# Padding the moving operands of the merge and of both MLP products by 64 bytes

## The chip, the cores and the metric

The kernel runs on one core of a Trainium2 chip. The metric is the device time of one execution in microseconds; lower is better. The time before is 3025.41 us, the median of 3 runs (3019.31 to 3026.27).

## The reference

One decoder layer on a sequence of 512 tokens with 2048 channels, in float32. What matters here is its dense part:

```
gates  = sigmoid(z[..., o_gate:] + gate_bias)            # three gates of 2048 channels
merged = g_a*(y_a @ wu[:768]) + g_b*(y_b @ wu[768:1408]) + g_c*(y_c @ wu[1408:])
x = x + merged @ w_out                                   # 2048 x 2048
h = rmsnorm(x, norm_mlp)
x = x + square(relu(h @ mlp_w1)) @ mlp_w2                # 2048 -> 8192 -> 2048
return rmsnorm(x, final_norm)
```

Ahead of it stand an input projection and three token mixers (S5, RWKV-7, gated linear attention), which the change doesn't touch.

## The kernel before, in words

Activations lie transposed, channels on the 128 partitions and the 512 tokens in the free direction, so that a weight tile of 128 x 128 is the standing operand of TensorE and an activation tile the moving one. Every operand of a dense product is split in two float32r tiles, a high part and the rest (`hl`, lines 875 to 877: ScalarE casts, VectorE subtracts). A product of two such pairs is three matmuls: high weights by high activations, high weights by low activations, low weights by high activations (`gemm`, L749 to L751, and `w1_mm`, L802). TensorE's order is the order of the program (`manual_schedule`); the other engines and the queue of SyncE, which issues the loads, are put in order by a planner.

The stages that the change touches come last:

- **The merge** (`up`): 16 output blocks of 16 weight tiles, moving operands `yh`/`yl`, 512 columns. 768 matmuls. The product with `w_out` (`wo`) follows, also 768, from tiles `mh`/`ml` that the change leaves alone.
- **The first MLP product** is done with seven quarter products in place of eight, numbered 1, 5, 6, 3, 7, 2, 4, on 256 columns: 32 units of seven products of 24 matmuls. The moving operands of 1, 5, 6 and 3 lie in one pair of tiles `hA` of the form [128, 8, 4, 256]: for each of 8 blocks k of channels the four operands side by side. They are written while `w_out` runs. Those of 7, 2 and 4 (`hB7`, `hB2`, `hB4`) are tiles of their own, filled at the start of this stage from DRAM through the staging tag `hraw` (L1264): six loads of 512 KB, each split by ScalarE and VectorE.
- **The second MLP product** (`w`): 8 chunks c of the hidden layer, each with 16 output blocks of 8 weight tiles. Its moving operands are `ah`/`al`, each a tile of 1024 columns that holds two operands; tag with 8 buffers, of which a chunk uses four. 2880 matmuls of 512 columns, and at the end 384 of 256.

A step in the free direction is 4 bytes, so a tile of 512 columns is 2048 bytes in each partition. In the program before every tile size above is a multiple of 512 bytes, hence all operands of a stage begin at the same remainder modulo 512. The program's addresses are: weights `whi`/`wlo` at 288, and a weight tile inside begins at a multiple of 512 behind it; `yh`, `yl`, `mh`, `ml`, `uh`, `ul` and the `hB` tiles at 288 too; `hA`, `ah`, `al` and the small tiles `tw`, `ta` of the RWKV preparation (L761 to L763) at 480. The distance of the moving operand's begin from the standing operand's is therefore 0 modulo 512 for `up`, `wo`, `z`, `gt` and `hB`, and 192 for `hA`, `w`, `pw` and `pa`.

Of the kernel before, what the change touches and what calls it, by code (L numbers as in the profile page):

```python
# [7 lines left out]
F32 = mybir.dt.float32  # L8
F32R = mybir.dt.float32r
# [4 lines left out]
P = 128  # L14
T = 512
# [705 lines left out]
class Trunk(K):  # L721
# [181 lines left out]
    def main(self, d, out):  # L903
# [8 lines left out]
        with tc.tile_pool(name="const", bufs=1) as cp, \  # L912
# [9 lines left out]
            def mixpool(name, side=None):  # L922
                return tc.tile_pool(name=name, bufs=1, reuse_waits="tile", side=side)
# [18 lines left out]
            with tc.manual_schedule(engines={mybir.EngineType.PE}):  # L942

                R = cp.tile([P, T], F32, name="R")
                u = []
# [143 lines left out]
                with mixpool("s5a") as sp, mixpool("rprep") as rp:  # L1089
# [14 lines left out]
                    for q in range(2):  # L1104
# [3 lines left out]
                        t = dr.tile([P, T], F32, name=f"tgd{q}")  # L1108
# [47 lines left out]
                m = []  # L1156
                with mixpool("merge") as mp:

                    yt = {j: [mp.tile([P, T], F32R, name=f"y{q}{j}") for q in "hl"] for j in (0, 1, 2, 3, 4, 5, 13, 14, 15)}
                    g0 = [mp.tile([P, T], F32, name=f"gl0_{q}", tag=f"gl{q}", bufs=2) for q in range(3)]  # L1160
                    yy = []
                    for j in list(range(6, NT)) + list(range(6)):
                        t = mp.tile([P, T], F32, name=f"yt{j}", tag="yt", bufs=4)
                        nc.sync.dma_start(t, yd[j])
                        if j not in yt:
                            yt[j] = [mp.tile([P, T], F32R, name=f"y{q}{j}") for q in "hl"]
                        self.hl(t, *yt[j])
                        yy.append(yt[j])
                    for j in range(NT):
                        gt = []  # L1170
                        for q in range(3):
                            t = mp.tile([P, T], F32, name=f"gl{j}_{q}", tag=f"gl{q}", bufs=2) if j else g0[q]
                            nc.sync.dma_start(t, gd[3 * j + q])
                            gt.append(t)
                        pp = [self.ps(f"up{j}_{q}") for q in range(3)]
                        self.run(self.gemm(f"up{j}", d["w_up"][j], [(pp[1], 5), (pp[2], 5), (pp[0], 6)], yy))
                        for q in (1, 2, 0):
                            self.mul(gt[q], gt[q], pp[q])
                        self.add(gt[1], gt[1], gt[2], nc.gpsimd)
                        self.add(gt[0], gt[0], gt[1])  # L1180
                        hi = ap.tile([P, T], F32R, name=f"mh{j}", tag="act")
                        lo = ap.tile([P, T], F32R, name=f"ml{j}", tag="act")
                        self.hl(gt[0], hi, lo)
                        m.append((hi, lo))
# [1 line left out]
                HA = (1, 5, 6, 3)  # L1186
                upper, front = contextlib.ExitStack(), contextlib.ExitStack()
                hp = upper.enter_context(mixpool("hcu", "right"))
                hA = [hp.tile([P, 8, 4, 256], F32R, name=f"hA{q}") for q in "hl"]
                hc = {i: [t[:, :, n] for t in hA] for n, i in enumerate(HA)}  # L1190
                fp = front.enter_context(mixpool("front", "right"))
                x1d = [dr.tile([P, T], F32, name=f"x1d{j}") for j in range(NT)]
# [43 lines left out]
                mp = lower.enter_context(mixpool("w1"))  # L1236
# [20 lines left out]
                with mixpool("hraw", "right") as rp:  # L1257
                    for n, i in ((2, 4), (1, 2), (0, 7)):
                        hc[i] = [mp.tile([P, 8, 256], F32R, name=f"hB{i}{q}") for q in "hl"]
                    for n, i in enumerate((7, 2, 4)):  # L1260
                        with tc.high_priority(self.wprio):
                            for h in range(2):
                                t = rp.tile([P, 4, 256], F32, name=f"hraw{i}{h}", tag="hraw", bufs=3)
                                nc.sync.dma_start(t, d3[:, n, 4 * h:4 * h + 4])  # L1264
                                self.hl(t, *(q[:, 4 * h:4 * h + 4] for q in hc[i]))
                    for n, (i, *w) in enumerate(gen):
                        self.w1_mm(bank[self.BANK[i]], i, w, hc, range(8))
                        self.w1_out(0, i, bank, keep, mp, R2, hid)
                        if n == 1:
                            pm = self.gps("pms")  # L1270
                            nc.tensor.matmul(pm, self.onesD, acc, start=True, stop=True)
                            self.ts(R2, pm, 1e-6, ALU.add)
                            nc.vector.reciprocal(R2, R2)
# [9 lines left out]
                with contextlib.ExitStack() as st:  # L1283
                    mp, hp = (st.enter_context(mixpool(n)) for n in ("x1b", "nrm"))
                    self.stg = st.enter_context(tc.tile_pool(name="sq", bufs=3, reuse_waits="tile"))
                    sq2 = hp.tile([P, T], F32, name="sq2")
                    gap = st.enter_context(mixpool("gap"))
                    gap.tile([P, 20 * 256], F32, name="gap")
                    rp = st.enter_context(mixpool("hr"))
                    xp = st.enter_context(mixpool("ah", "right"))  # L1290
                    acc2 = hp.tile([P, T], F32, name="acc2")
# [2 lines left out]
                    def hidden(u):  # L1294

                        with tc.high_priority(2 * self.wprio):
                            t = rp.tile([P, 1024], F32, name=f"hr{u}", tag="hr", bufs=3)
                            nc.sync.dma_start(t, hid[u])
                            r = [xp.tile([P, 1024], F32R, name=f"a{q}{u}", tag=f"a{q}", bufs=8) for q in "hl"]
                            self.hl(t, *r)  # L1300
                        return [tuple(x[:, T * q:T * q + T] for x in r) for q in range(2)]
                    nxt = [a for u in range(4) for a in hidden(u)]
                    xq = [mp.tile([P, 4, T], F32, name=f"x1b{j}") for j in range(NT // 4)]
                    x1 = [xq[j // 4][:, j % 4] for j in range(NT)]
# [7 lines left out]
                    for c in range(8):  # L1312
                        aa, nxt = nxt, []

                        pts = [bank8(f"w2_{c}_{j}") for j in range(2)]
                        gens = [self.gemm(f"w2_{c}_{j}", d["w2"][c, j], [(pts[j], 8)], aa) for j in range(2)]
                        for gen in gens:
                            for _ in range(3):
                                next(gen)
                        for j in range(NT if c < 7 else NT // 2):  # L1320
                            if j < 2:
                                pt = pts[j]
                                self.run(gens[j])
                            else:
                                pt = bank8(f"w2_{c}_{j}")
                                self.run(self.gemm(f"w2_{c}_{j}", d["w2"][c, j], [(pt, 8)], aa))
                            self.add(x1[j], x1[j], pt)
                            if c < 7 and j in (2, 4, 6, 8):
                                nxt += hidden(4 * c + 3 + j // 2)
                            if c == 7:  # L1330
                                self.sumsq(acc2, x1[j], j)
                                nc.scalar.activation(x1[j], x1[j], AF.Copy, scale=col("final", j))
# [130 lines left out]
```

## Time and profile before

| | |
|---|---|
| median of 3 runs | 3025.41 us |
| profiled execution, its own time | 3027.89 us |
| its span, first to last instruction | 3025.8 us |
| TensorE matmul busy | 2957.4 us (98%) |
| TensorE weight load busy | 2518.7 us (83%), overlaps the matmuls |
| VectorE / ScalarE / GpSimd busy | 61% / 38% / 11% |
| mean granted clock of TensorE | 0.987 |

A matmul's duration in the profile contains what it shares with its neighbours, as they are pipelined: a row says 0.39 us where the next one begins 0.23 us later. What a matmul costs in a row of them is the distance between two starts, called pitch here.

### The profile page before, as it was taken

Reading aid. Unit: us, or ns where it says so; the run is one execution under the profiler, and the core shown is the slowest. Engines: PE = TensorE matmul, PEld = TensorE weight load, DVE = VectorE, ACT = ScalarE, POOL = GpSimd, SP = SyncE. Lnnn points to the kernel's source line nnn. Section 1 sums busy time; section 2 is a strip of 40 time slices with the busy share of each in tenths; the row PEclk is TensorE's granted clock in tenths of the full one; section 3 lists DMA queues with packets and bytes.
Section 4 is the critical chain, followed back from the end, with each engine's and each line's share of the span. In section 5 each row is a group of like instructions: output and inputs, shape, how many; then the busy total and the mean of one; then the engine's idle time right before and its main releaser. Section 6 shows DMA issues by size and latency. Waiting matters only on the chain.

```text
span 3025.8 us, 41943 instructions
## 1 busy us (share of the span) xinstructions
PE 2957.4 (98%) x16447; PEld 2518.7 (83%) x16447; DVE 1830.8 (61%) x2574; ACT 1160.5 (38%) x1434; POOL 325.8 (11%) x560
## 2 busy tenths in 40 slices
PE   8999989899999999999999999999999999999997
PEld 7888777778877777888888999999998888888887
DVE  7766888855673554655445877777775434333436
ACT  6554222234563142432233555555554222222225
POOL 1001666630000000001011000000000000000002
PEclk9999989999999999999999999999999999999999
DMA  5345433445337262655554644454546333233224
GB/s 183 126 162 176 125 105 96 127 130 168 103 98 192 72 175 69 228 168 170 158 162 151 218 160 161 161 168 161 168 141 236 118 125 112 104 118 125 98 98 146
DMA packets 195605, 436.08 MB, mean 144 GB/s; under 512 B 66096, under 2 KB 80176, under 8 KB 194608
## 3 DMA queue, kind: packets, MB, share of 16 engines
q1 hardware_dynamic: 195408, 433.40, 44.4%
q8 instruction: 129, 2.11, 0.3%
q14 instruction: 68, 0.56, 0.1%
HBM read 359.70 MB, written 68.70 MB: 142 GB/s over the span
## 4 chain that ended last, share of the span: by engine, by line
PE 84%; DVE 7%; POOL 3%; DMA 2%; issue 2%; SPq 1%; ACT 1%; DVEq 0%; ACTq 0%; POOLq 0%
PE ha L802 12%; PE w L749 8%; PE w L750 8%; PE w L751 8%; PE hc L802 6%; PE gt L749 6%; PE gt L751 5%; PE gt L750 5%; PE hb L802 3%; PE z L749 2%; PE z L751 2%; PE z L750 2%; PE wo L750 2%; PE up L751 2%; PE up L750 2%; PE wo L749 2%
## 5 line engine op out<-in xcount | busy, mean ns | idle before, releaser
L751 PE MATMUL w<-ah,wlw 128*128 128x512 f32 (+1 forms) x1088 | 413.9, 380 | 1.2 <-DVE wlw L33 1.2
L749 PE MATMUL w<-ah,whw 128*128 128x512 f32 (+1 forms) x1088 | 413.8, 380 | 0.0
L750 PE MATMUL w<-al,whw 128*128 128x512 f32 (+1 forms) x1088 | 413.6, 380 | 0.0
L732 ACT CAST whw<-wrw 128x1024 fp32r<-128x1024 f32 x136 | 142.5, 1048 | 495.1 <-PE w L750 493.5
L30 DVE TENSOR_TENSOR x1b<-x1b,w 128x512 f32<-128x512 f32 (+1 forms) x136 | 89.1, 655 | 384.8 <-PE w L751 375.2
L749 PE MATMUL gt<-uh,whgt 128*128 128x512 f32 x768 | 311.7, 406 | 1.2 <-DVE gz L27 1.2
L751 PE MATMUL gt<-uh,wlgt 128*128 128x512 f32 x768 | 301.4, 392 | 3.6 <-DVE wlgt L33 3.6
L750 PE MATMUL gt<-ul,whgt 128*128 128x512 f32 x768 | 301.1, 392 | 0.0
L749 PE MATMUL z<-uh,whin 128*128 128x512 f32 x608 | 244.6, 402 | 10.3 <-DVE zs L27 10.3
L751 PE MATMUL z<-uh,wlin 128*128 128x512 f32 x608 | 241.6, 397 | 8.1 <-DVE wlin L33 8.1
L751 PEld LDWEIGHTS w<-ah,wlw 128*128 128x128 f32 x1088 | 203.6, 187 | 46.1 <-DVE wlw L33 1.6
L750 PE MATMUL z<-ul,whin 128*128 128x512 f32 x608 | 240.8, 396 | 0.0
L749 PEld LDWEIGHTS w<-ah,whw 128*128 128x128 f32 x1088 | 203.6, 187 | 44.5
L750 PEld LDWEIGHTS w<-al,whw 128*128 128x128 f32 x1088 | 203.6, 187 | 44.5
L732 ACT CAST whgt<-wrgt 128x1024 fp32r<-128x1024 f32 x96 | 100.2, 1046 | 271.0 <-PE gt L750 162.9
L793 ACT CAST whu<-wAu 128x1024 fp32r<-128x1024 f32 x128 | 133.7, 1045 | 159.3 <-DVE wAu L30 82.5
L33 DVE TENSOR_TENSOR wlu<-wAu,whu 128x1024 fp32r<-128x1024 f32 x128 | 156.4, 1222 | 44.9 <-ACT whu L793 44.9
L33 DVE TENSOR_TENSOR wlw<-wrw,whw 128x1024 fp32r<-128x1024 f32 x136 | 168.7, 1241 | 20.5 <-ACT whw L732 20.5
L751 PEld LDWEIGHTS gt<-uh,wlgt 128*128 128x128 f32 x768 | 145.0, 189 | 36.7 <-DVE wlgt L33 5.3
L749 PEld LDWEIGHTS gt<-uh,whgt 128*128 128x128 f32 x768 | 144.8, 189 | 36.5 <-issue 2.5
L750 PEld LDWEIGHTS gt<-ul,whgt 128*128 128x128 f32 x768 | 145.2, 189 | 27.2
L30 POOL TENSOR_TENSOR acc<-acc,sq 128x512 f32<-128x512 f32 x14 | 22.9, 1635 | 1327.3 <-ACT sq L896 1297.2
(495 smaller groups left out, 7061.8 us busy)
## 6 DMA issues: line engine op xcount, KB each, us to landing
wrw<-in_w SPq DMA_DIRECT2D x136, 512.0 KB, 3.2
wrgt<-in_w_in SPq DMA_DIRECT2D x96, 512.0 KB, 4.3
wrin<-in_w_in SPq DMA_DIRECT2D x76, 512.0 KB, 3.9
wrup<-in_w_up SPq DMA_DIRECT2D x32, 512.0 KB, 4.3
wrwo<-in_w_out SPq DMA_DIRECT2D x32, 512.0 KB, 3.9
wAu<-in_w SPq DMA_DIRECT2D x32, 512.0 KB, 5.5
wDu<-in_w SPq DMA_DIRECT2D x32, 512.0 KB, 3.8
wBu<-in_w SPq DMA_DIRECT2D x32, 512.0 KB, 4.3
```

The lines of the kernel that those rows point to most:

```text
L30: (eng or self.nc.vector).tensor_tensor(out, a, b, ALU.add)
L33: (eng or self.nc.vector).tensor_tensor(out, a, b, ALU.subtract)
L732: nc.scalar.copy(hi, raw)
L749: nc.tensor.matmul(ps, hi[:, ws], xh, start=first, stop=False)
L750: nc.tensor.matmul(ps, hi[:, ws], xl, start=False, stop=False)
L751: nc.tensor.matmul(ps, lo[:, ws], xh, start=False, stop=last)
L793: nc.scalar.copy(hi, x)
L802: self.nc.tensor.matmul(ps, w[a][:, ws], hc[i][b][:, k], start=i in (1, 5, 2) and k == 0 and q == 0, stop=k == 7 and q == 2, skip_group_ch ...
```

## The change

The moving operands get 16 unused columns (64 bytes) behind them. The tiles of the merge become 512 + 16 columns long, `hA`'s inner rows 256 + 16, and `ah`/`al` 1024 + 16. Whatever reads or writes them sees the same columns as before. As neighbours now lie at steps of 2112, 1088 and 4160 bytes, which leave 64 modulo 512, the operands of a stage begin at up to eight remainders modulo 512 in steps of 64. For the room, the staging tag `hraw` goes from 3 buffers to 2, and the unused tile `gap`, which only sets where the following pool begins, shrinks by 1 KB in each partition.

```diff
-                    yt = {j: [mp.tile([P, T], F32R, name=f"y{q}{j}") for q in "hl"] for j in (0, 1, 2, 3, 4, 5, 13, 14, 15)}
+                    shifted = lambda j: [mp.tile([P, T + 16], F32R, name=f"y{q}{j}")[:, 0:T] for q in "hl"]
+                    yt = {j: shifted(j) for j in (0, 1, 2, 3, 4, 5, 13, 14, 15)}
...
-                            yt[j] = [mp.tile([P, T], F32R, name=f"y{q}{j}") for q in "hl"]
+                            yt[j] = shifted(j)
...
-                hA = [hp.tile([P, 8, 4, 256], F32R, name=f"hA{q}") for q in "hl"]
+                hA = [hp.tile([P, 8, 4, 272], F32R, name=f"hA{q}")[:, :, :, 0:256] for q in "hl"]
...
-                                t = rp.tile([P, 4, 256], F32, name=f"hraw{i}{h}", tag="hraw", bufs=3)
+                                t = rp.tile([P, 4, 256], F32, name=f"hraw{i}{h}", tag="hraw", bufs=2)
...
-                    gap.tile([P, 20 * 256], F32, name="gap")
+                    gap.tile([P, 19 * 256], F32, name="gap")
...
-                            r = [xp.tile([P, 1024], F32R, name=f"a{q}{u}", tag=f"a{q}", bufs=8) for q in "hl"]
+                            r = [xp.tile([P, 1040], F32R, name=f"a{q}{u}", tag=f"a{q}", bufs=8)[:, 0:1024] for q in "hl"]
```

## Rows read from the trace of the kernel before

**Rows 1.** The page: engines' busy time, the granted clock, the chain by engine.
```profile
PE 2957.4 (98%) x16447; PEld 2518.7 (83%) x16447; DVE 1830.8 (61%) x2574; ACT 1160.5 (38%) x1434; POOL 325.8 (11%) x560
...
PEclk9999989999999999999999999999999999999999
...
PE 84%; DVE 7%; POOL 3%; DMA 2%; issue 2%; SPq 1%; ACT 1%; DVEq 0%; ACTq 0%; POOLq 0%
```

**Rows 2.** Busy time by stretch: merge, first product, second product, its end; (x) counts instructions.
```profile
1303.50:1477.60 174.10, 174.10 (x769) 144.14 (x768) 88.82 (x110) 43.67 (x48) 20.43 (x16) 1.00 0.52 162
1652.00:2290.00 638.00, 630.33 (x5385) 628.13 (x5384) 505.25 (x495) 343.14 (x427) 1.45 (x1) 1.00 0.50 167
2290.00:2962.00 672.00, 672.00 (x2884) 538.61 (x2883) 263.18 (x271) 167.03 (x167) 9.55 (x6) 1.00 0.36 124
2962.00:3011.00 49.00, 45.52 (x389) 44.47 (x387) 36.67 (x49) 33.31 (x53) 16.30 (x9) 1.00 0.48 161
```

**Rows 3.** Timeline of TensorE, single matmuls: start, duration, line, tiles.
```profile
1304.66 0.39 PE L749 MATMUL up<-yh,whup 128*128 128x512 f32 x1
...
1310.79 0.39 PE L749 MATMUL up<-yh,whup 128*128 128x512 f32 x1
...
2102.58 0.28 PE L802 MATMUL hc<-hAh,whu 128*128 128x256 f32 x1
...
2105.30 0.28 PE L802 MATMUL ha<-hB7h,whu 128*128 128x256 f32 x1
...
2108.16 0.28 PE L802 MATMUL hb<-hB2h,whu 128*128 128x256 f32 x1
...
2111.04 0.28 PE L802 MATMUL ha<-hB4h,whu 128*128 128x256 f32 x1
...
2113.92 0.29 PE L802 MATMUL ha<-hAh,whu 128*128 128x256 f32 x1
...
2116.66 0.28 PE L802 MATMUL hc<-hAh,whu 128*128 128x256 f32 x1
...
2399.74 0.39 PE L750 MATMUL w<-al,whw 128*128 128x512 f32 x1
...
2405.81 0.39 PE L749 MATMUL w<-ah,whw 128*128 128x512 f32 x1
```

**Rows 4.** Timeline of TensorE where two small products stand between input products.
```profile
95.60 0.39 PE L750 MATMUL z<-ul,whin 128*128 128x512 f32 x1
...
96.05 0.39 PE L761 MATMUL pw<-twh,whwa 128*128 128x512 f32 x1
...
97.45 0.39 PE L749 MATMUL z<-uh,whin 128*128 128x512 f32 x1
...
98.61 0.39 PE L751 MATMUL z<-uh,wlin 128*128 128x512 f32 x1
...
99.97 0.39 PE L751 MATMUL z<-uh,wlin 128*128 128x512 f32 x1
```

**Rows 5.** The tile hraw: its loads, and their time to landing.
```profile
L1264 SPq DMA_DIRECT2D hraw<-d x6: 319/326/423, 1657.7 to 1669.9; - x6
...
DMA to landing us min/median/max: 4.0/8.0/11.1
```

**Rows 6.** Timeline of SyncE's queue and of VectorE at the first product's start.
```profile
1657.70 2.09 SPq L1264 DMA_DIRECT2D hraw<-d  x3
...
1664.05 3.95 SPq L1264 DMA_DIRECT2D hraw<-d  x2
...
1669.94 0.32 SPq L1264 DMA_DIRECT2D hraw<-d  x1
...
1680.10 2.35 DVE L33 TENSOR_TENSOR hB4l<-hraw,hB4h 128x1024 fp32r<-128x1024 f32 x2
```

**Rows 7.** Whom TensorE waited for, in all: total us, times, longest.
```profile
PE hb L802 <- ACT whu L793: 3.3, 1, 3.3
...
PE ha L802 <- DVE hB4l L33: 0.2, 1, 0.2
```

## The prediction

> **What bounds the kernel now.** I read the page first. TensorE's matmuls are busy for 98% of the span and have 84% of the chain that ended last, and its granted clock is full in nearly every slice [rows 1]. So a change counts only as far as it moves TensorE's pitch or makes it wait. Next come the stages that the diff touches, in the view by stretches [rows 2]: the merge holds 769 matmuls in 174.1 us and the second product 2884 in 672.0 us, both with TensorE busy throughout, and the first product 5385 in 638.0 us with under 8 us idle. [...] No load, cast or eviction ends last there; the pitch itself is the cost.
>
> Then the single matmuls [rows 3]. They show that matmuls of one shape don't have one pitch:
>
> - `up`, 512 columns, distance 0: 1304.66 to 1310.79 is 27 steps, 226.9 ns each (the stretch in [rows 2] gives 226.4).
> - `w`, 512 columns, distance 192: 2399.74 to 2405.81 is 26 steps, 233.4 ns.
> - `hc` from `hA`, 256 columns, distance 192: 2102.58 to 2105.30 is 24 steps, 113.3 ns.
> - `hB2`, 256 columns, distance 0: 2108.16 to 2111.04 is 24 steps, 120.0 ns.
>
> Shape, engine, clock and the weights' addresses are the same inside each pair; what differs is where the moving operand begins against the standing one. So the distance is worth 6.7 ns a matmul, and with opposite sign for the two widths: 192 is the bad one for 512 columns and the good one for 256. Whether that is a matter of both addresses or of the moving one alone can't be told here, since all weights begin at one remainder.
>
> [rows 4] show what a change of distance does on the way. Input products run at distance 0; then six matmuls `pw`, `pa` at distance 192 (96.05 to 97.45) take 1.40 us, 233.3 ns each from the first on; back at distance 0 the next five take 1.16 us (97.45 to 98.61), 232 ns each, and only then does the pitch fall to 226.7 ns (six in 98.61 to 99.97). A run at the other distance is thus entered at once, while the way back to 0 costs about five matmuls.
>
> **The change part by part.** After it, the operands of a stage begin at 0, 64, ..., 448 modulo 512. The trace holds just 0 and 192 in long runs. I assume that what counts is the distance modulo 128, so that even multiples of 64 behave as 0 and odd ones as 192. That is a choice: it is the shortest period in which the two measured kinds differ on this grid. No run of matmuls in these rows lies under 226.7 ns at 512 columns or 113.3 at 256, so no stage is let go below that, and a stage that has it today can only lose.
>
> *Merge, 768 matmuls.* `yh` now begins at even multiples, `yl` at odd ones, so each triple goes 0, 64, 0. It leaves the best pitch known for 512 columns. Lower end: 226.7 as now, 0 us. Upper end: 233.4, 768 x 6.7 ns = 5.1 us. Since the distance changes with every matmul, I take the pitch of the five that follow a change, nearly 231 to 232: 768 x 4.3 ns = +3.3 us.
>
> *First product, 3072 matmuls on `hA`.* Operand n of block k begins at 192 + 64n + 256k: products 1 and 6 (n = 0, 2) keep the good kind, 5 and 3 (n = 1, 3) get the bad one, for all 24 matmuls of a product. What such a run costs behind one at 192 stands in [rows 3]: `hB7`, 2105.30 to 2108.16, is 24 steps of 119.2 ns. So 1536 x 5.9 ns = 9.1 us. Product 7, which then follows one of its own kind, goes from 119.2 to 120.0: 768 x 0.8 = 0.6 us. Product 6, now entered from the bad kind, is what product 1 is today: 2113.92 to 2116.66, 24 steps of 114.2 ns against 113.3, 768 x 0.9 = 0.7 us. Sum +10.4 us. Lower end 0 us (all new distances as good as 192), upper end 3072 x 6.7 = +20.6 us. `hB2`, `hB7` and `hB4`, which have the bad distance today, aren't touched.
>
> *Second product, 2880 matmuls.* Buffer b of `ah` and of `al` is shifted by 64b alike, so six matmuls in a row share a distance and the kind alternates with each buffer. It leaves the bad distance. If the half that becomes good were good at once, 1440 x 6.7 ns = -9.6 us. With the five slow ones of [rows 4] in each run of six, that run takes 1.16 + 0.227 = 1.387 us in place of 1.400, only 2.2 ns a matmul: 1440 x 2.2 = -3.2 us. I take the middle, -6.4 us. Outer ends: 0 us, and -19.3 us if all eight distances gave 226.7.
>
> *Its end, 384 matmuls of 256 columns* (the last stretch of [rows 2]), distance 192 today, half of them turned bad: 192 x 6.7 = +1.3 us; ends 0 and +2.6.
>
> *`hraw` from 3 buffers to 2.* Before, the first three loads go out together at 1657.70, the fourth and fifth behind the release of a buffer at 1664.05 and after, the sixth at 1669.94 [rows 6]; a load lands 4.0 to 11.1 us after its issue [rows 5]. With two buffers the third waits for the first release, 1664.05, so some 5 us later, and the last two follow it. [...] The last splits end at 1682.45 today (1680.10 + 2.35 [rows 6]), and TensorE waits 0.2 us for them [rows 7]: there is no cover left at that end. What hides part of it is the 3.3 us wait for weights just ahead [rows 7], in which the third operand isn't wanted either. Ends: -3.3 us if the later loads let those weights land sooner and that wait goes, and +6 us if the whole delay shows; I take +2 us, near the cover.
>
> *Nothing for the rest.* The same casts and subtractions write the same columns. On `hA` three blocks of 256 lie 1088 bytes apart in place of 1024, beside the `w_out` product, where VectorE and ScalarE have room [rows 1]; if that cover were gone, the delay could show only in the first waits of the first product. `gap` issues no instruction.
>
> Sum: 3.3 + 10.4 - 6.4 + 1.3 + 2.0 = +10.6 us. The profiled execution took 3027.89 us, 2.1 more than its span and 2.5 above the median shown; it becomes 3038.5, and on the median 3036.0.
>
> [...]
>
> **The rivals.**
>
> *The distance is not what sets the pitch.* The 6.7 ns could come from something that the stages differ in besides (which tiles, which engines write next to them, the number of weight loads in flight). For it: no run of the trace has the same tiles at two distances. Against it: `pw`, `pa` change to 233.3 ns in the midst of input products and back. Time: only `hraw`, 3025.4 + 2.0 = 3027. Chance 0.20.
>
> *Most new distances are good for both widths* (the faster side). Only one remainder in eight would be bad for a width: 192 for 512 columns, 0 for 256. Then seven eighths of `w` drop to 226.7, 2520 x 6.7 = -16.9 us; an eighth of `up` gets worse, +0.6; an eighth of `hA`, +2.6; end +0.3; `hraw` +2. Sum -11.4, 3014. It decides from the point where `w` averages below about 229.4 ns, as then its gain passes 11.5 us, and `hA` stays below 116. For it: the trace knows six remainders on the grid not at all. Against it: entering 0 from 192 costs five slow matmuls even where 0 is good. Chance 0.18.
>
> *Many distances never settle.* Each change of distance starts the slow steps anew, `hA` goes to the 120.0 ns of `hB` throughout and `up` to 233.4, while `w` gains nothing: 20.6 + 5.1 + 2.6 + 2 = +30, 3055. For it: the five slow matmuls. Against it: entering 192 costs nothing. Chance 0.10.
>
> The forecast has 0.52: its own range is 3028 to 3045, from `w` at -9.6 or -3.2, `hraw` at 0 or 6, and half as much on `hA`.
>
> **How the numbers follow.** A measurement of this kernel tells some 0.3%, 9 us, from no change: 3016 to 3034.5 counts as the same. Faster: the second rival's 0.18 nearly whole, 0.16. Same: the first rival's 0.20, and about a third of the forecast, where `hA` costs less, in all 0.38. Slower: the rest of the forecast and the third rival, 0.46. The range for 8 in 10 takes in the first rival, most of the second and the near part of the third: 3011 to 3049.
>
> **What would show it.** In the changed trace: `w` averaging 230 to 232 ns a matmul (the same stretch near 666 us in place of 672); `up` near 231; `ha`/`hc` of products 5 and 3 at 119 to 120 with 1 and 6 at 113 to 114; the waits of `hb` and `ha` on `hraw`'s splits longer by some 2 us. The prediction is wrong in its assumption if products 5 and 3 differ between even and odd k, or if 1 and 6 move; wrong in its sign if `w` falls to 227 while `hA` stays at 113.

## The result, and the profile after

The changed kernel takes 3057.49 us (median of 4 runs, 3055.87 to 3059.69) against 3024.23 of the kernel before, measured beside it. The ratio is 1.0113, with a 95% interval of 1.0095 to 1.013: 33 us slower. Slower was the forecast too, but by less: 3036.0 us, with a range that ended at 3049.

The page of the profiled execution (span 3054.0 us, its own time 3055.87), with the lines that answer to [rows 1]:

```profile
PE 2972.4 (97%) x16447; PEld 2536.6 (83%) x16447; DVE 1831.3 (60%) x2574; ACT 1160.7 (38%) x1434; POOL 326.1 (11%) x560
...
PE 83%; DVE 7%; DMA 3%; POOL 3%; issue 2%; SPq 1%; ACT 1%; DVEq 0%; ACTq 0%; POOLq 0%
```

The instructions are the same in number. TensorE's matmuls are busy 15.0 us longer, the span is 28.2 us longer: about half of the loss is longer matmuls, half is waiting. The view by stretches places it. Each stretch is cut at the first matmul of its stage; the columns are the stretch, its length, the busy time of TensorE's matmuls, of its weight loads, of VectorE, ScalarE and GpSimd, the granted clock and the DMA share with GB/s. The kernel before, cut finer than [rows 2] (unit 0 of the first product, units 1 to 30, the last unit, the second product):

```profile
1652.83:1684.22 31.39, 23.72 (x172) 21.72 (x170) 26.67 (x27) 15.61 (x20) 1.45 (x1) 0.95 0.72 256
1684.22:2270.08 585.86, 585.86 (x5042) 585.86 (x5041) 461.23 (x451) 314.00 (x391) 0.00 (x0) 1.00 0.49 163
2270.08:2289.60 19.52, 19.52 (x170) 19.52 (x169) 16.94 (x18) 13.19 (x16) 0.00 (x0) 1.00 0.48 163
2289.60:2961.61 672.01, 672.01 (x2882) 538.57 (x2881) 263.39 (x270) 166.98 (x167) 9.55 (x6) 1.00 0.36 124
```

The changed kernel, the merge ahead of these four:

```profile
1301.34:1478.95 177.61, 177.61 (x770) 144.11 (x769) 88.84 (x110) 43.53 (x48) 20.58 (x16) 1.00 0.51 159
1653.07:1690.42 37.35, 26.58 (x172) 24.19 (x170) 29.23 (x29) 16.30 (x20) 1.46 (x1) 0.86 0.66 229
1690.42:2287.62 597.20, 597.20 (x5043) 597.20 (x5041) 458.79 (x449) 312.97 (x390) 0.00 (x0) 1.00 0.47 156
2287.62:2318.63 31.01, 20.07 (x171) 19.86 (x169) 16.98 (x18) 14.91 (x18) 0.00 (x0) 0.88 0.54 187
2318.63:2989.30 670.67, 670.20 (x2880) 542.74 (x2881) 263.85 (x270) 166.25 (x165) 9.96 (x6) 1.00 0.36 123
```

Merge and units 1 to 30 are longer with TensorE busy throughout: that is pitch. Unit 0 and the last unit hold idle time, 10.8 and 10.9 us, where they had 7.7 and none. The last unit's matmuls end after 20.07 us; the idle time behind them counts to its stretch, which ends where the second product begins. That stretch is the surprise: nothing was forecast there. The waits of TensorE name what ends each (total us, times, longest; they answer to [rows 7]):

```profile
PE w L749 <- ACT ah L876: 10.9, 1, 10.9
...
PE hb L802 <- ACT hB2h L876: 2.6, 1, 2.6
PE hb L802 <- DVE hB2l L33: 2.1, 1, 2.1
...
PE ha L802 <- ACT hB4h L876: 1.3, 1, 1.3
...
PE ha L802 <- DVE hB4l L33: 0.9, 1, 0.9
```

The first is new: the second product's first matmul waits 10.9 us for the cast of its first operand. That cast waits for a load of the hidden layer, `hr<-hid`, line 1299 after and 1298 before. SyncE's queue in the kernel before (two more loads go at 1710.67 and 1730.19, so that the three buffers of `hr` are filled long ahead; the loads at 2285.04 fill them again):

```profile
1691.87 0.33 SPq L1298 DMA_DIRECT2D hr<-hid  x1
...
2285.04 2.92 SPq L1298 DMA_DIRECT2D hr<-hid  x3
...
2298.16 0.32 SPq L828 DMA_DIRECT2D hid<-hy  x1
```

and in the changed one, where no such load stands ahead of 2312.80:

```profile
2291.67 0.33 SPq L828 DMA_DIRECT2D hid<-hy  x1
2296.21 14.05 SPq L729 DMA_DIRECT2D wrw<-in_w  x6
2312.38 0.33 SPq L828 DMA_DIRECT2D hid<-hy  x1
2312.80 1.77 SPq L1299 DMA_DIRECT2D hr<-hid  x3
```

Before, the loads of the first chunk go out ahead of the last store of the hidden layer, `hid<-hy`, and TensorE doesn't wait for their casts. After, they stand behind that store, which needs the last unit's results: what was a prefetch, three of its four loads over 550 us early, comes after its consumer is free.

The wait costs more than its length. In the first 6.37 us of the second product, behind the 10.9 us of idling, the granted clock is 0.51:

```profile
2318.63:2325.00 6.37, 5.90 (x13) 4.32 (x14) 3.65 (x3) 2.09 (x2) 0.00 (x0) 0.51 1.05 397
```

Most matmuls begin 427 ns apart there, and the first 24 take 3.4 us more than in the run below that has the same paddings without the wait.

The same boundaries give this table (us, change against the kernel before; the three columns on the right are experiments told below). The product with `w_out` is unchanged to 0.1 in all of them.

| stage | forecast | changed kernel | paddings of merge and second product alone | padded `hA`, `hraw` at 2 | `gap` alone |
|---|---|---|---|---|---|
| merge | +3.3 | +3.52 | +3.52 | 0 | 0 |
| first product, unit 0 | +2.0 | +5.95 | -0.17 | +3.33 | -0.49 |
| units 1 to 30 | +10.4 | +11.34 | 0 | +11.33 | -0.01 |
| last unit | 0 | +11.49 | 0 | +0.38 | +11.31 |
| second product | -6.4 | -1.33 | -4.69 | +2.51 | +2.61 |
| its end | +1.3 | +0.55 | +0.57 | +1.02 | +0.96 |

The changed stages together are 31.5 us longer. The gate product, which the change doesn't touch, was 3.5 us shorter in this profiled execution than in that of before; over the runs below it lies between 735.5 and 741.6. That is why the two profiled executions differ by only 28 us.

The columns don't add up stage by stage. The three experiments together give 2.67 us for unit 0 and 2.55 for the end, where the changed kernel has 5.95 and 0.55. The end also moved by 0.96 with `gap` alone, where no operand of TensorE moved.

### The profile page after: what moved, and what is told of

Its sections match the earlier page's. It is cut to its first block, busy times and chain, and to the rows that moved or that the text cites. A ratio compares the mean times of both kernels' runs of the same rounds, so it can differ in the third digit from the quotient of the medians.

```text
span 3054.0 us, 41951 instructions
## 1 busy us (share of the span) xinstructions
PE 2972.4 (97%) x16447; PEld 2536.6 (83%) x16447; DVE 1831.3 (60%) x2574; ACT 1160.7 (38%) x1434; POOL 326.1 (11%) x560
## 4 chain that ended last, share of the span: by engine, by line
PE 83%; DVE 7%; DMA 3%; POOL 3%; issue 2%; SPq 1%; ACT 1%; DVEq 0%; ACTq 0%; POOLq 0%
PE ha L802 12%; PE w L750 8%; PE w L749 8%; PE w L751 8%; PE hc L802 6%; PE gt L749 5%; PE gt L751 5%; PE gt L750 5%; PE hb L802 3%; PE z L749 2%; PE z L751 2%; PE z L750 2%; PE up L751 2%; PE up L750 2%; PE up L749 2%; PE wo L750 2%
## 5 line engine op out<-in xcount | busy, mean ns | idle before, releaser
L749 PE MATMUL w<-ah,whw 128*128 128x512 f32 (+1 forms) x1088 | 415.3, 382 | 10.9 <-ACT ah L876 10.9
```

Source lines behind the costliest of these rows:

```text
L749: nc.tensor.matmul(ps, hi[:, ws], xh, start=first, stop=False)
```

## The experiments

**The unused tile alone.** The kernel before, with nothing but this:

```diff
-                    gap.tile([P, 20 * 256], F32, name="gap")
+                    gap.tile([P, 19 * 256], F32, name="gap")
```

> The kernel before with one edit: the unused tile gap 1 KB smaller, so that the buffers hr of the second product begin 1 KB lower and the first of them lies on a buffer of pk6, which the first product's last unit still reads. No operand of TensorE moves. Theory A (the lost prefetch): the loads of hr for the first chunk go out only behind that read, TensorE waits some 11 us before the first matmul of w; 12 to 16 us slower than before. Theory B (the late loads come from hA's growth, which pushes the tile wA under the third buffer of hr, and gap is harmless): within 2 us of before, and no wait over 1 us at the start of w.

3039.3 us (3037.08 to 3042.99, 4 runs) against 3026.45 (13 runs), ratio 1.0045 [1.003, 1.006]. The last unit is 11.31 us longer, the second product 2.61, and the wait is the one of the changed kernel:

```profile
PE w L749 <- ACT ah L876: 11.2, 1, 11.2
```

So theory A holds: a tile that no instruction touches costs 13 us by its size. By the program's addresses, `gap` ends where the three buffers of `hr` begin: at 133408 before, at 132384 after. There the second buffer of `pk6` lies (132384 to 133408), a copy that the last unit of the first product still reads. What holds the load back at last is its place in SyncE's queue. In the changed kernel VectorE's last read of `pk6` begins at 2299.1 and takes 0.4 us:

```profile
L33 DVE TENSOR_TENSOR hy<-hc,pk x32: 415/424/425, 1670.4 to 2299.1; 128x256 f32<-128x256 f32 x32
```

The load goes out 13 us later, at 2312.80, 0.1 us after the queue is done with the last store (2312.38 and 0.33 long). The overlap moved the load to another place in the queue's order, which the planner sets; why this is behind the store and not only behind the read isn't shown. The 2.61 us in the second product lie in its first 24 matmuls, as above.

**The staging tag alone.** The kernel before, with:

```diff
-                                t = rp.tile([P, 4, 256], F32, name=f"hraw{i}{h}", tag="hraw", bufs=3)
+                                t = rp.tile([P, 4, 256], F32, name=f"hraw{i}{h}", tag="hraw", bufs=2)
```

> The kernel before with one edit: hraw with 2 buffers in place of 3. Theory A: this alone makes the first unit of the first product 5 to 6 us longer, through waits of hb and ha for hB2 and hB4; 3029 to 3031 us on the median. Theory B (the waits in the changed kernel come from its slower matmuls and other order): under 2 us.

3031.18 us (10 runs), ratio 1.0012 [1.0003, 1.0021]; unit 0 is 3.52 us longer, the other stages of the table unchanged to 0.3. In unit 0 neither number was met: more than B's, less than A's; the median lies 4.7 us up, at A's upper end, with an interval of 0.9 to 6.4. The waits are A's: TensorE now waits 6.3 us for the splits of `hB2` and `hB4`, partly in place of other waits. The longest new wait is this one (the kernel before has no row for it):

```profile
PE hb L802 <- ACT hB2h L876: 3.8, 1, 3.8
```

**The unused tile put back.** The changed kernel, with `gap` at 20 * 256 again:

```diff
-                    gap.tile([P, 19 * 256], F32, name="gap")
+                    gap.tile([P, 20 * 256], F32, name="gap")
```

> The changed kernel with one edit back: gap at its old size. hr then begins behind pk6 again, but its third buffer still lies on wA, which hA's growth pushed down. Theory A (gap alone lost the prefetch): the wait of 10.9 us at the start of w goes, 11 to 15 us faster than the changed kernel, 3042 to 3046. Theory B (wA's overlap is enough to lose it): as the changed kernel, 3055 to 3060.

3046.63 us (4 runs), ratio to before 1.0063 [1.0048, 1.0078], some 11 us less than the changed kernel, a little under A's gain. The last unit is back at 19.91 us and the wait at the second product's start is gone, as A said, though the first `hr` load still goes out late, 6.4 us ahead of that start (2305.0; the second product begins at 2311.43):

```profile
L1299 SPq DMA_DIRECT2D hr<-hid x32: 319/323/652, 2305.0 to 2845.2; - x32
```

So a lead of 6.4 us is enough for the first matmul there (1.0 us of waiting is left behind it); in the changed kernel the load goes 5.1 us behind the end of the last unit's matmuls (2287.62 + 20.07), and TensorE waits 10.9.

**The second product at distance 0.** The kernel before, with 192 unused bytes behind `ah` and `al`, which lowers their addresses by as much, so that both begin at the weights' remainder:

```diff
                     nxt = [a for u in range(4) for a in hidden(u)]
+                    xp.tile([P, 48], F32, name="space")
```

> The kernel before with one edit: 192 unused bytes behind ah and al, so that both begin at 288 modulo 512, the remainder of the weights, all buffers alike: distance 0 in place of 192. Theory A (the distance of the moving from the standing operand sets the pitch, two kinds): w at 226.7 ns, its 256-column end at about 120; 2880 x 6.7 - 384 x 6.7 = 16.7 us faster, 3007 on the median. Theory B (the pitch belongs to the stage, not to the distance): w stays at 233.3, within 2 us of before.

3008.05 us (3003.59 to 3011.22, 4 runs), ratio 0.9944 [0.9927, 0.996]. The second product falls by 19.18 us, 226.7 ns a matmul in place of 233.3:

```profile
2283.58:2936.41 652.83, 652.83 (x2883) 540.55 (x2881) 264.07 (x271) 167.56 (x167) 9.65 (x6) 1.00 0.38 128
```

The premise of the prediction, that distance sets the pitch, holds so far; the moving operand's address alone is not yet excluded.

**The weights moved instead.** The kernel before, with 192 unused bytes ahead of the weights. They and all tiles on their side of memory move by 192, `hA`, `ah` and `al` do not: these keep their addresses and change their distance, while the merge and the `hB` tiles keep their distance and change their addresses.

```diff
+            wp.tile([P, 48], F32, name="wspace")
```

> The kernel before with 192 unused bytes ahead of the weight tiles: the weights and everything on the left side of SBUF begin at 480 in place of 288 modulo 512, the right side (hA, ah, al) stays at 480. The moving operands of w and of hA keep their addresses, only the weights move: distance 192 becomes 0; hB, up and wo keep distance 0 at new addresses. Theory A (the distance between the two operands counts): w 226.7 ns, hA 120.0, up, wo and hB as before; -19.2 + 20.5 + 0.9 us, about +2 in all. Theory B (the moving operand's own address counts): w 233.3 and hA 113.3 as before, while up and wo, now at 480, go to 233.3 and hB to 113.3.

3024.77 us against 3022.66, one execution each. The merge, units 1 to 30 and the second product by stretch:

```profile
1300.60:1474.68 174.08, 174.08 (x770) 144.17 (x768) 88.84 (x110) 43.70 (x48) 20.46 (x16) 1.00 0.52 162
1679.78:2284.58 604.80, 604.80 (x5043) 604.80 (x5042) 461.19 (x451) 313.63 (x391) 0.00 (x0) 1.00 0.47 158
2304.74:2957.56 652.82, 652.82 (x2882) 540.83 (x2881) 263.23 (x270) 167.73 (x167) 9.67 (x6) 1.00 0.38 128
```

The merge is where it was, the second product is 19.2 us shorter, units 1 to 30 are 18.9 longer. Starts of four of the seven products of a unit, 24 matmuls each, as in [rows 3]:

```profile
2002.34 0.28 PE L802 MATMUL ha<-hAh,whu 128*128 128x256 f32 x1
...
2005.21 0.28 PE L802 MATMUL hc<-hAh,whu 128*128 128x256 f32 x1
...
2016.73 0.28 PE L802 MATMUL hb<-hB2h,whu 128*128 128x256 f32 x1
...
2019.62 0.28 PE L802 MATMUL ha<-hB4h,whu 128*128 128x256 f32 x1
```

`hA` at its old address takes 2.87 us for 24 matmuls, about 120 ns, where it took 2.72 [rows 3]; `hB2` at a new address still takes 2.89. Only the distance goes with all of these, theory A; one execution is enough for that, as each pitch is the mean of hundreds of matmuls.

**Three maps of distances.** The kernel before, with unused bytes ahead of `yh`/`yl` and of each `hB` tile and behind `ah`/`al`, and as much on `gap` as the `hB` tiles got. The first map:

```diff
+                    mp.tile([P, 16], F32, name="spacey")
...
+                        if (c := {4: 16, 2: 16, 7: 32}[i]):
+                            mp.tile([P, c], F32, name=f"space{i}")
...
-                    gap.tile([P, 20 * 256], F32, name="gap")
+                    gap.tile([P, 20 * 256 + 64], F32, name="gap")
...
+                    xp.tile([P, 16], F32, name="space")
```

> The kernel before with unused bytes ahead of some moving operands, each stage at one distance: hB4 64, hB2 128, hB7 256, ah and al 128, yh and yl 64 (others as before). Theory A (period 128, two kinds on the grid of 64): hB4 113.3 ns, hB2 and hB7 120.0, w 226.7, up 233.3. Theory C (a period of 512, in which each distance has a pitch of its own): some of them off these values by more than 1 ns.

> As the run map1 with other distances: hB4 320, hB2 384, hB7 448, ah and al 256, yh and yl 384. Theory A: hB4 and hB7 113.3 ns, hB2 120.0, w 226.7, up 226.7. Theory C: some of them off these values by more than 1 ns.

> As the run map1 with distances off the grid of 64: hB4 32, hB2 96, hB7 160, ah and al 32, yh and yl 96. Theory A says nothing of them but that 32 and 160 are alike (128 apart). From the one step at such a distance in the trace of before (pvr, spl: 1070.40 to 1070.63 and the steps after it near 233), 512 columns at 32 would be at 228 to 238 ns, 256 columns at 113 to 120. A better distance than both known ones would show as w or up under 226 or a hB under 113.

The second has 96, 80, 16, 16 and 112 columns in these places, the third 24, 8, 16, 16 and 40. The distances in the three maps are 64, 384 and 96 for the merge, 64, 320 and 32 for `hB4`, 128, 384 and 96 for `hB2`, 256, 448 and 160 for `hB7`, 128, 256 and 32 for the second product. Times 3020.97, 3023.11 and 3026.95 against 3022.66, one execution each. Mean pitch in ns by distance, from the starts of all matmuls of a stage:

| distance | 256 columns | 512 columns |
|---|---|---|
| 0 | 120.0 | 226.7 |
| 32 | 116.6 | 233.3 |
| 64 | 117.7 | 228.9 |
| 96 | 119.8 | 233.4 |
| 128 | 118.9 | 232.4 |
| 160 | 117.3 | not tried |
| 192 | 113.3 or 117.8 | 233.3 |
| 256 | 119.2, behind 192 as 0 | 226.7 |
| 320 | 117.7 | not tried |
| 384 | 119.8 | 233.3 |
| 448 | 117.8 | not tried |

Theory A, the period of 128 of the prediction, falls: 64 is not 192, 128 is not 0. 256 acts as 0, 320 has the pitch of 64, and 384 is 0.9 ns off 128; 448 was tried only behind products at 117.8, but product 1 of the changed kernel, which alternates 192 and 448 from block to block, keeps its 114.13 ns. So distances 256 apart are nearly alike, though not all of them quite. No distance tried lies below 113.3 or 226.7. And in the second map `hA`, at its unchanged 192, ran at 117.8:

```profile
2005.23 0.28 PE L802 MATMUL ha<-hAh,whu 128*128 128x256 f32 x1
...
2008.06 0.28 PE L802 MATMUL hc<-hAh,whu 128*128 128x256 f32 x1
...
2010.89 0.28 PE L802 MATMUL ha<-hAh,whu 128*128 128x256 f32 x1
```

Each product takes 2.83 us there against 2.72 in [rows 3]. It is entered from `hB4`, at 320 in this map and at 0 before; entered from 64 in the first map and from 32 in the third, it kept 113.3.

**The change without `hA`.** The changed kernel with `hA`, `hraw` and `gap` as before: the paddings of the merge and of the second product alone.

```diff
-                hA = [hp.tile([P, 8, 4, 272], F32R, name=f"hA{q}")[:, :, :, 0:256] for q in "hl"]
+                hA = [hp.tile([P, 8, 4, 256], F32R, name=f"hA{q}") for q in "hl"]
```

> The changed kernel without its change to hA, and so with hraw at 3 buffers and gap at its old size: the paddings of the merge and of the second product alone. Theory A (these stages cost what their pitches say, and the waits come with hA's room): merge +3.5 us, w -3 to -4.7, its end +0.6; within 2 us of before. Theory B (the paddings themselves cost the time): half or more of the 33 us, 3040 or more.

3025.67 us (11 runs) against 3025.92 (15), ratio 0.9999 [0.999, 1.0008]. By stage it is the third column of the table above: the gain on the second product pays for the merge.

**`hA` without the rest.** The kernel before with the padded `hA` and `hraw` at 2 buffers:

```diff
-                hA = [hp.tile([P, 8, 4, 256], F32R, name=f"hA{q}") for q in "hl"]
+                hA = [hp.tile([P, 8, 4, 272], F32R, name=f"hA{q}")[:, :, :, 0:256] for q in "hl"]
```

> The kernel before with hA padded, and for the room hraw with 2 buffers; gap at its old size. Theory A: +11.3 us in the units 1 to 30 of the first product by the pitch of products 5, 3 and 6, +5.7 in its unit 0 by hraw, +0.4 in its last unit, the rest as before; 3040 to 3044 on the median. Theory B (the pitches of a stage hang on the ones before it, so without the merge's padding the first product differs): the units 1 to 30 off +11.3 by more than 2 us.

3045.58 us (5 runs), ratio 1.0065 [1.0051, 1.0079], a little over A's upper end. Units 1 to 30 are A's, +11.33, so B falls; unit 0 is less than A's, 3.33 in place of 5.7, and the second product, which A left as it was, is 2.51 us longer. There TensorE is idle for 1.7 us, in three waits for splits of `al`, where it had no gap before. By the program's addresses the larger `hA` moves `wA`, the first product's weights, over the third buffer of `hr`, and the first `hr` loads go out at 2291.84 in place of 1691.87, 6.5 us ahead of the second product. So a late load is the likely cause; it wasn't tried by itself. In sum the loss is accounted for: -0.3 of the paddings, +19.7 here, +12.9 of `gap` make 32.3, and 33.3 were measured. By stage it is not quite, as the table shows: unit 0 has 3.3 us more than the three together, the second product and its end 3.8 less.

**All at 192, and a reset kept.** If 192 is the good distance for 256 columns, every `hB` tile should go there, together with the second product at 0. The kernel before with:

```diff
+                        if (c := {4: 48, 2: 0, 7: 0}[i]):
+                            mp.tile([P, c], F32, name=f"space{i}")
...
-                    gap.tile([P, 20 * 256], F32, name="gap")
+                    gap.tile([P, 20 * 256 + 48], F32, name="gap")
...
+                    xp.tile([P, 48], F32, name="space")
```

> The kernel before with all operands of a stage at the one distance that is best for its width: ah and al at distance 0 (unused bytes behind them), hB4, hB2 and hB7 at 192 like hA (unused bytes ahead of them, gap grown by as much). Theory A (one distance for a long row beats many): w 226.7 ns, hA and hB 113.3; 19.2 - 0.9 us from the second product and 2304 x 6.7 = 15.4 us from the first, 2989 to 2993 on the median. Theory B (at distance 192 the pitch of 256 columns hangs on how the row is entered, and with no product at distance 0 between them all seven products stay at the 117.8 ns that the run map2 shows): first product 5376 matmuls, 3072 x 4.4 - 2304 x 2.2 = +8.4 us; 3013 to 3017.

3015.86 us (5 runs), ratio 0.9964 [0.9952, 0.9977]: all seven products average 117.6 to 117.9 ns over units 1 to 30, and these lost 7.61 us. Theory B's number is met: at 192 the pitch depends on what ran before. But it does not take another distance to lose the good pitch. These are the starts of products 3, 7, 2 and 4 of unit 1:

```profile
1690.59 0.28 PE L802 MATMUL hc<-hAh,whu 128*128 128x256 f32 x1
...
1693.31 0.28 PE L802 MATMUL ha<-hB7h,whu 128*128 128x256 f32 x1
...
1696.24 0.28 PE L802 MATMUL hb<-hB2h,whu 128*128 128x256 f32 x1
...
1699.07 0.28 PE L802 MATMUL ha<-hB4h,whu 128*128 128x256 f32 x1
```

Product 3 still takes 2.72 us, 113.3 ns. In product 7 one step takes 226 ns, twice the usual, and from there on every product to the end of unit 31 runs at 117.8, product 2 with its 2.83 us as the first whole one. A step of 221 ns at the begin of product 6 had not done that. So one tile, `hB4`, stays at 0 ahead of `hA`, and `hB2` and `hB7` go to 192:

```diff
-                        if (c := {4: 48, 2: 0, 7: 0}[i]):
+                        if (c := {4: 0, 2: 48, 7: 0}[i]):
```

> The run best with one edit: hB4, the last product of each unit, stays at distance 0, so hA, hB7 and hB2 are at 192 and each row of six products is entered from a product at 0, as hA is in the kernel before. Theory A (at 192 the pitch of 256 columns hangs on the entry: from 0 it settles at 113.3, and stays there as long as the distance does): products 1, 5, 6, 3, 7, 2 at 113.3, 4 at 120; first product 1536 x 6.7 = 10.2 us below before, second as in best, 18.3 below; 2996 to 2999 on the median. Theory B (the 117.7 ns come with where hB7 and hB2 lie, whatever ran before): products 7 and 2 at 117.8, the first product 3 to 8 us longer than before; 3010 to 3016.

2997.1 us (2994.84 to 2998.32, 4 runs) against 3026.57 (7 runs), ratio 0.9901 [0.9885, 0.9918]: 29 us faster than the kernel before and 60 than the changed one. Units 1 to 30 and the second product:

```profile
1681.84:2258.32 576.48, 576.48 (x5043) 576.48 (x5042) 461.09 (x451) 314.04 (x391) 0.00 (x0) 1.00 0.49 165
2277.52:2930.34 652.82, 652.82 (x2882) 540.55 (x2881) 264.25 (x271) 167.76 (x167) 9.67 (x6) 1.00 0.38 128
```

and the starts of the products that show the reset:

```profile
2000.41 0.28 PE L802 MATMUL ha<-hB7h,whu 128*128 128x256 f32 x1
...
2003.13 0.28 PE L802 MATMUL hb<-hB2h,whu 128*128 128x256 f32 x1
...
2005.86 0.28 PE L802 MATMUL ha<-hB4h,whu 128*128 128x256 f32 x1
...
2008.72 0.29 PE L802 MATMUL ha<-hAh,whu 128*128 128x256 f32 x1
```

`hB7` and `hB2` at 192 take 2.72 and 2.73 us, 113.3 ns; `hB4` at 0 costs 2.86, and buys the good pitch for the six products behind it.

## Why the prediction was wrong in size

**`gap` issues no instruction: the step that failed.** It was costed at nothing because it does no work. But its size is an address, and the address decides over whose memory `hr` comes to lie. The experiment with it alone gives 11.31 us in the last unit and 2.61 in the second product, more than any other term, and the largest part of what the sum lacks. The prediction had asked of each moved step what it waits for, and not of a resized tile whom its neighbour now waits for. "Nothing for the rest" missed the same for the growth of `hA`, which put `wA` under the third buffer of `hr`; with `gap` at its old size that experiment lost 2.51 us in the second product.

**`hraw`: mis-sized.** Forecast +2, with an upper end of +6; alone it measured +3.52, in the changed kernel +5.95. The third load no longer goes with the first two, as forecast, but the last pair goes at 1678.47, not near 1670 [rows 6]:

```profile
1657.95 1.62 SPq L1265 DMA_DIRECT2D hraw<-d  x2
...
1664.32 5.36 SPq L1265 DMA_DIRECT2D hraw<-d  x2
...
1678.47 1.46 SPq L1265 DMA_DIRECT2D hraw<-d  x2
```

With two buffers the last pair needs the split of the middle pair, of which the first ends at 1678.4, so the delay is not one release but two in a row, 1664.32 and 1678.47:

```profile
L33 DVE TENSOR_TENSOR hB2l<-hraw,hB2h x2: 1216/1216/1217, 1677.2 to 1678.4; 128x1024 fp32r<-128x1024 f32 x2
```

Half of the 5.95 isn't waiting: of the stretch, 3.1 us are idle and 2.9 are matmuls that took longer, at a granted clock of 0.86 in place of 0.95. Why this is 2.4 us more than with `hraw` alone stays open; the changed kernel with `gap` put back has it too (+5.66), the padded `hA` with two buffers has not (+3.33). As far as single profiled executions tell, it goes with the other paddings, which alone cost unit 0 nothing (-0.17); but unit 0 moved by -1.25 us also in the experiment on `ah`/`al`, which doesn't touch it.

**First product: the sum near, its parts not, and in part by luck.** +10.4 was forecast for `hA` over 32 units and +11.34 measured over 30. Starts of the products of one unit of the changed kernel, in the order 1, 5, 6, 3, 7, and the begin of 2:

```profile
2008.93 0.29 PE L802 MATMUL ha<-hAh,whu 128*128 128x256 f32 x1
...
2011.66 0.28 PE L802 MATMUL hc<-hAh,whu 128*128 128x256 f32 x1
...
2014.53 0.28 PE L802 MATMUL ha<-hAh,whu 128*128 128x256 f32 x1
...
2017.36 0.28 PE L802 MATMUL hc<-hAh,whu 128*128 128x256 f32 x1
...
2020.20 0.28 PE L802 MATMUL ha<-hB7h,whu 128*128 128x256 f32 x1
...
2023.07 0.28 PE L802 MATMUL hb<-hB2h,whu 128*128 128x256 f32 x1
```

Product 5 takes 2.87 us for 24 matmuls; over units 1 to 31 it averages 119.20 ns, forecast 119.2. Product 1 stays good at 114.13. Product 6, forecast good at 114.2, runs at 117.95: it lies at 64 and 320, which are not 192. This is the sign of a wrong assumption that the prediction itself named. It costs 768 x 3.75 ns = 2.9 us more; product 3, 118.51 in place of 119.2, and 7, 119.65 in place of 120.0, give 0.8 back. So the period of 128 was wrong; that the sum came near all the same is in part luck, since only product 6 lies where the wrong assumption costs much.

**Merge and second product.** The merge came as forecast, 231.3 ns and +3.52. The second product's pitch fell to 231.7 ns, as forecast in kind, but that is 4.69 us where nothing else disturbs it and not 6.4; the late loads, through the clock of 0.51 behind their wait, took 3.4 us of the changed kernel's gain back. Its end was +0.55 for +1.3.

**The rivals.** That the distance has no part in the pitch is refuted by the weights' move: the second product and the products on `hA` kept their addresses and changed from 233.3 to 226.7 ns and from 113.3 to 120.0. The distance is worth 19 us of one stage here (the second product's 672.01 us against 652.82); what makes it count, no run here shows. That most new distances are good is refuted by the map: besides 0 and 256, the 512-column pitch is best at 64, with 228.9. The third rival's 3055 comes near the measured time, but not on its way: `hA` did not go to 120.0 throughout, nor the merge to 233.4, and the second product did gain.

## What to carry to other kernels

Ask of every resized tile, used or not, which tiles change their address and over whose last reader they then lie; a prefetch that slips behind its predecessor's last store leaves its load and cast uncovered, here 11 us for 1 KB, however early it went out before. Where a stage has TensorE busy throughout and matmuls of one shape show two pitches (here 226.7 and 233.3 ns), compare the begins of moving and standing operands, and move a single tile to test it. Take one good distance per width from the trace rather than spread the operands over many. Then read the pitch again: 512 columns kept theirs at distance 0, 226.7 ns, but 256 columns, all at the good 192, lost 7.6 us over units 1 to 30 and gained 9.4 only with one product of seven left at 0.

## What was not expected of the hardware

The pitch at distance 192 with 256 columns has two values, 113.3 and 117.8 ns, and it holds the one that it has over whole products and units. It was 113.3 behind products at 0, 32 and 64, and 117.8 behind one at 320. With all seven products at 192, the first products of unit 1 still had 113.3, lost it behind one step of 226 ns, and no product of units 2 to 31 came back to it. In the kernel before, too, products 6 and 3 of unit 1 went to 117.8 behind one step of 161 ns, and in unit 2, behind products at 0, `hA` ran at 113.3 again. With `gap` alone changed, the 256-column matmuls of the second product's end ran at 117.4 ns in place of 113.8 at an unmoved distance. One product in seven at 0, itself slower (2.86 us for 24 matmuls against 2.72), is worth 17 us there (593.47 against 576.48 over units 1 to 30). Since 64 and 320 have the same pitch, 117.7 ns, but hand on a different one, the distance of the product ahead doesn't settle it alone, and a long step can change it with no change of distance; what settles it is open.
